# A hybrid attention layer on one core: an order that counts ScalarE's table loads, negated scores in one attention, and four token tiles in a weight buffer

## The chip, the cores and the metric

The kernel runs on 1 core of one Trainium2 chip. The metric is the time of one execution in microseconds (us) of device time, as the median of several runs; less is better. Beside it stands one execution recorded by the hardware profiler, with start and end of every instruction. The engines are PE (TensorE: matmuls and transposes; PEld is its weight load), DVE (VectorE), ACT (ScalarE), POOL (GpSimd) and SP (SyncE, which issues the DMAs here).

## The reference

One layer, applied to a prompt of 1024 tokens and to a sample of 32 tokens that has a cache of 512 older ones; model width 1024, all in float32. There are two attentions with 8 heads of 64 each: A is a softmax over a band of chunks with a learnt position bias, B is "stick-breaking", which is made of sigmoids and a running product.

```python
hn = rmsnorm(h, g_pre)
qA, kA, vA, gA, qB, kB, vB, gB = split(hn @ w_in)        # 8 times 512 columns
# A, per head: keys of the own 64-token chunk and the 8 chunks before
s  = qA @ kA.T * 64**-0.5 + bias[clip(k_pos - q_pos, -128, 128)]
oA = softmax(where(band, s, -1e30)) @ vA
# B, per head, strictly causal
z  = qB @ kB.T * 64**-0.5
after = sum over later causal keys of log_sigmoid(-z)
oB = where(causal, exp(log_sigmoid(z) + after), 0) @ vB
y  = concat(oA * silu(gA), oB * silu(gB)) @ w_out
h  = h + rmsnorm(y, g_post)
h  = h + sigmoid(h @ w_ple_gate) * (p @ w_ple)
```

The new keys and values are outputs too.

## The kernel before, in words

Tokens are taken as 9 tiles of 128 (the last holds the 32 of the sample); for the input projection they are regrouped into 3 column chunks of 352. Every float32 operand of a large matmul is split into a rounded high part and a low rest (`hi`, `lo`), and a product is three matmuls: high by high, high by low, low by high.

The work has three parts. **The start** (to about 60 us) loads the token tiles x0 to x8 (`load_x`), squares and scales them (`scale_x`), transposes them (`turn_x`) and makes the first projections qA, kA, vA of head pair 0. Tiles x0 to x2 and the later ones live in `ring0`, an arena with room for three such tiles; x3 and x4 live in a buffer `x34` that has the tag `wTh`, the place where the transposed attention weights go later. **The attention part** (to about 600 us) goes through eight stages, one for each pair of heads, in the order A0 B0 A1 B1 A2 B2 A3 B3. Within a stage two heads of one attention run (`attention`), while the projections of the next stage (or, in the last one, the gates) run between them as the dense work. In two A stages and two B stages the sample's attention is put in (`sample_attention`). **The last part** makes w_out and w_ple_gate with a seven-product Strassen scheme.

For one unit of attention, that is a head and a block of 128 queries, the steps are: scores on PE into one or two PSUM banks (tag `S`, three banks in all); in A, DVE adds the bias and takes the row maximum in one instruction (`tensor_tensor_reduce`, shown as CUSTOM_DVE_ANT_0 with its accumulator read), DVE negates that maximum, ACT takes the exponential with the negated maximum as bias, DVE takes a reciprocal, POOL multiplies; in B, ACT takes two sigmoids of the bank, DVE runs a product scan backwards over it, POOL multiplies. Then PE transposes the weights (`ptw`), ACT rounds them (`wTh`), DVE makes the rest (`wTl`), and PE multiplies with the values (`PV`).

ACT evaluates exponentials and sigmoids from tables, and an ACT_TABLE_LOAD stands in its queue wherever the one follows the other. Copies, casts and squares need no load of their own here.

The order of instructions is not that of the Python code. A `Recorder` takes down every operation with what it depends on, a planner (`order`) then simulates the five engines with fixed costs (`cost`) and emits for each engine a fixed queue: at each step the engine that can start first takes the ready operation of the lowest key, and on PE attention has class 0 and dense work class 1, so dense work fills the time in which no attention matmul is ready. An operation on another engine is counted as ready for PE only 400 ns late (`MARGIN`). All operations are emitted from one line of a helper, so the profile shows the one line L450 for nearly all of them and groups are told apart by the names of tiles.

Of the kernel before, what the change touches and what calls it, by code (L numbers as in the profile page):

```python
# [10 lines left out]
AF = mybir.ActivationFunctionType  # L11
ALU = mybir.AluOpType

P = 128
D = 1024
# [7 lines left out]
HD = 64  # L23
NEG = -1e30
# [148 lines left out]


class Op:
    __slots__ = ("eng", "what", "args", "kw", "key", "busy", "late", "ready", "left", "after", "at", "size", "shared")


LAND = {"PE": 165, "ACT": 0, "DVE": 0, "POOL": 0, "SP": 0, "CTL": 0}
SEM = 60  # L180
MARGIN = 400
ISSUE = 550
DMA_NS, DMA_RATE, DMA_MARGIN = 1500, 320.0, 2000
DVE_SET, POOL_SET = 137, 110

# [78 lines left out]
class Recorder:  # L264


    def __init__(self):
        self.ops, self.cls, self.low, self.closed, self.turns = [], 0, 0, [], []
        self.tensor = Engine(self, "PE", "tensor")
        self.vector = Engine(self, "DVE", "vector")  # L270
        self.scalar = Engine(self, "ACT", "scalar")
        self.gpsimd = Engine(self, "POOL", "gpsimd")
        self.sync = Engine(self, "SP", "sync")
# [26 lines left out]
    def node(self, eng, what, args, kw, after):  # L300
        o = Op()
        o.eng, o.what, o.args, o.kw, o.after = eng, what, args, kw, after
        o.key = (self.cls if eng == "PE" else self.low, len(self.ops))
        o.shared = False
        self.ops.append(o)
        return o

    def add(self, eng, what, args, kw):
        writes, reads = [], []
        method = what[1] if isinstance(what, tuple) else ""  # L310
        for i, a in enumerate(args):
            if isinstance(a, (View, Raw, Segments)):
                (writes if i == 0 or (method == "tensor_tensor_reduce" and i == 7) else reads).append(a)
        for k, a in kw.items():
            if isinstance(a, (View, Raw, Segments)):
                (writes if k in ("out", "accum_out") else reads).append(a)
        o = self.node(eng, what, args, kw, set())
        for mine, write in ((reads, False), (writes, True)):
            for v in mine:
                b = v.buf  # L320
                hit = False
                for other, box, wrote in b.uses:
                    if other is not o and (write or wrote) and all(p < y and x < q for (p, q), (x, y) in zip(v.box, box)):
                        o.after.add(other)
                        hit = True
                if b.pool is not None:
                    if not hit:
                        o.after.add(b.place)
                    b.pool.ops.append(o)
                b.uses.append((o, v.box, write))  # L330
        o.busy, o.late = self.cost(eng, method, args, kw, writes, reads)
        o.shared = eng == "POOL"
        if eng == "DVE":
            sbuf = [v for v in reads if isinstance(v, (View, Segments)) and not v.buf.psum and v.free() > 4]
            o.shared = len(sbuf) > 1 or (method == "tensor_copy" and len(sbuf) == 1 and not writes[0].buf.psum)
# [36 lines left out]
    def order(self):  # L372

        import heapq
        for place, old in self.turns:
            place.after.update(x[0] for x in old.uses)
        users = {id(o): [] for o in self.ops}
        for o in self.ops:
            o.left, o.ready = len(o.after), 0.0
            for a in o.after:  # L380
                users[id(a)].append(o)
        names = ("PE", "ACT", "DVE", "POOL", "SP", "CTL")
        free = dict.fromkeys(names, 0.0)
        soon = {e: [] for e in names}
        now = {e: [] for e in names}
        for o in self.ops:
            if not o.left:
                heapq.heappush(soon[o.eng], (0.0, o.key, id(o), o))
        out, port, line = [], 0.0, 0.0
        while len(out) < len(self.ops):  # L390
            best = None
            for e in names:
                if now[e]:
                    t = free[e]
                elif soon[e]:
                    t = max(free[e], soon[e][0][0])
                else:
                    continue
                if best is None or t < best[0]:
                    best = (t, e)  # L400
            t, e = best
            while soon[e] and soon[e][0][0] <= t:
                _, key, n, o = heapq.heappop(soon[e])
                heapq.heappush(now[e], (key, n, o))
            o = heapq.heappop(now[e])[2]
            if o.shared and e == "DVE" and port > t + DVE_SET:
                held = [x for x in now[e] if not x[2].shared]
                if held:
                    heapq.heappush(now[e], (o.key, id(o), o))
                    pick = min(held)  # L410
                    now[e].remove(pick)
                    heapq.heapify(now[e])
                    o = pick[2]
            o.at = t
            if e == "CTL":
                done = t
            elif e == "SP":
                free[e] = t + o.busy
                line = max(line, t + o.busy + DMA_NS) + o.late
                done = line + DMA_MARGIN  # L420
            else:
                if o.shared:
                    t = max(t, port - (DVE_SET if e == "DVE" else POOL_SET))
                    port = t + o.busy
                free[e] = t + o.busy
                done = t + o.busy + o.late
            out.append(o)
            for u in users[id(o)]:
                if u.eng == e and e != "SP":
                    r = t if e == "CTL" else free[e]  # L430
                else:
                    r = done + (0 if u.eng == "CTL" else SEM + (MARGIN if u.eng == "PE" else 0))
                u.ready = max(u.ready, r)
                u.left -= 1
                if not u.left:
                    heapq.heappush(soon[u.eng], (u.ready, u.key, id(u), u))
        return out
# [18 lines left out]
def stream_step(  # L456
# [108 lines left out]
    def load_x(t):  # L565
        n = min(P, T - t * P)
        if t == 3:
            x34.append(at.tile([P, ringh.cols], F32, tag="wTh", name="x34"))
        xt = x34[0][:, (t - 3) * D:(t - 2) * D] if 3 <= t < 5 else ring0.tile([P, D], f"x{t}")
        dma(xt[0:n], x_prompt[0, t * P:t * P + n, :] if t < 8 else x_sample[0])  # L570
        return xt, n

# [33 lines left out]
    def bias_rows():  # L606

        rb = ring0.tile([8, 257], "rb")
        dma(rb, rel_bias[0])
        R = ring1.tile([8, 768], "R")  # L610
        nc.gpsimd.memset(R, 0.0)
        nc.vector.tensor_scalar(R[:, 256:768], R[:, 256:768], rb[:, 0:1], None, ALU.add)
        nc.vector.tensor_copy(R[:, 0:256], rb[:, 0:256][:, ::-1])
        dma(r_dr, R)

# [96 lines left out]
    def col_steps(j):  # L712
# [7 lines left out]
        def mms(c, part):  # L720
# [24 lines left out]
                nc.gpsimd.tensor_tensor(sg, sg, box["og"], ALU.mult)  # L745
                dma(og_dr[n, :, cs], sg)
            elif k == "q":
                nc.scalar.activation(box["st"][:, cs], acc, AF.Copy, scale=SCALE)
            else:
                nc.scalar.copy(box["st"][:, cs], acc)  # L750

# [26 lines left out]
    def attention(ab, p, h):  # L778
# [5 lines left out]
        def begin():  # L784
            if ab == "A":
                bias = at2.tile([P, 640], F32, tag="bias", name=f"bias{nm}", bufs=2)
                dma(bias, bias_src(2 * p + h, P, 0, 640))
                nc.gpsimd.memset(bias[0:HD, 0:HD], NEG)
                nc.gpsimd.memset(bias[HD:P, 576:640], NEG)
                box["bias"] = bias  # L790

        def lo_block(i):
# [20 lines left out]
        def scores(i):  # L813
# [27 lines left out]
            else:  # L841
                m = small.tile([P, 4], F32, tag="stat", name=f"stat{nm}_{i}", bufs=6)
                for j, (a, b, s) in enumerate(pieces):
                    nc.vector.tensor_tensor_reduce(
                        w0[:, a:b], s, box["bias"][:, n - b:n - a][:, ::-1], 1.0,
                        -3e38 if j == 0 else m[:, j - 1:j], ALU.add, ALU.max, m[:, j:j + 1])
                last = len(pieces) - 1
                nc.vector.tensor_scalar(m[:, 2:3], m[:, last:last + 1], -1.0, None, ALU.mult)
                nc.scalar.activation(w1[:, 0:n], w0[:, 0:n], AF.Exp, bias=m[:, 2:3], accum_out=m[:, 3:4])
                nc.vector.reciprocal(m[:, 3:4], m[:, 3:4])  # L850
                nc.gpsimd.tensor_scalar(w1[:, 0:n], w1[:, 0:n], m[:, 3:4], 1.0, ALU.mult, ALU.mult)
            state[i] = w0, w1
# [96 lines left out]
    def sample_attention(ab, gi):  # L949
# [45 lines left out]
        def scores():  # L995
# [20 lines left out]
            else:  # L1016
                m = small.tile([P, 4], F32, tag="stat", name="stat" + nm, bufs=6)
                for j, (a0, b0, s) in enumerate(pieces):
                    nc.vector.tensor_tensor_reduce(
                        w0[:, a0:b0], s, bx["bias"][:, NK - b0:NK - a0][:, ::-1], 1.0,  # L1020
                        -3e38 if j == 0 else m[:, 0:1], ALU.add, ALU.max, m[:, j:j + 1])
                nc.vector.tensor_scalar(m[:, 2:3], m[:, 1:2], -1.0, None, ALU.mult)
                nc.scalar.activation(w1[:, 0:NK], w0[:, 0:NK], AF.Exp, bias=m[:, 2:3], accum_out=m[:, 3:4])
                nc.vector.reciprocal(m[:, 3:4], m[:, 3:4])
                nc.gpsimd.tensor_scalar(w1[:, 0:NK], w1[:, 0:NK], m[:, 3:4], 1.0, ALU.mult, ALU.mult)
            bx["w1"] = w1
# [829 lines left out]
```

## Time and profile before

| | us |
|---|---|
| median of 3 runs (lowest to highest) | 794.32 (794.28 to 794.92) |
| time of the profiled execution | 794.5 |
| its span from the first to the last instruction | 792.7 |
| around the span | 1.8 |
| PE busy | 778.6 |
| ACT busy, DVE busy, POOL busy | 537.3, 587.4, 470.1 |

A busy time is the union of the recorded durations. A matmul's recorded end is modelled and lies later than the start of the next one, so that a short wait of PE hides in the overlap; the start times are what is measured. In a timeline row the first number is the start in us from the span's start, the second the duration in us, and the bracket at the end is the idle time before it and what ended it. In a group of instructions, "x12 | 15.4, 1283 | 0.9" is 12 instructions, 15.4 us together, 1283 ns on average and 0.9 us of idle time before them.

### The profile page before, as it was taken

How to read it: one execution, taken by the hardware profiler on the slowest of the kernel's cores; microseconds unless marked ns; L12 is line 12 of the kernel's file. 1: busy time of each engine (PE TensorE's matmuls, PEld its weight loads, DVE VectorE, ACT ScalarE, POOL GpSimd, SP SyncE). 2: the span in 40 equal slices, each digit the busy share in tenths (PEclk: the TensorE clock that was granted, in tenths of full speed). 3: DMA queues.
4: the chain of work that ended last, by engine and by line, in shares of the span. 5: the costliest groups of instructions: out<-in, count | busy, mean ns of one | idle time of the engine just before them, and what ended most of it. 6: DMA issues, size and time to landing. Idle time of an engine off the chain costs nothing.

```text
span 792.7 us, 14512 instructions
## 1 busy us (share of the span) xinstructions
PE 778.6 (98%) x4606; PEld 717.9 (91%) x4606; DVE 587.4 (74%) x1170; ACT 537.3 (68%) x1173; POOL 470.1 (59%) x554
## 2 busy tenths in 40 slices
PE   8999999999999999999999999999999999999997
PEld 7999999899989998999998999999998787888786
DVE  7717778787778686877867788767565677988965
ACT  6636786786797677887766778664436976777551
POOL 5625867675777677454635246657462529599533
PEclk9999999999999999999999999999999999999999
DMA  8419866767866858544514746756589866859853
GB/s 296 138 49 289 215 188 213 189 189 226 229 192 205 232 176 238 144 128 123 142 54 132 172 111 175 225 167 188 151 261 291 282 190 186 288 168 336 272 170 133
DMA packets 161087, 153.66 MB, mean 194 GB/s; under 512 B 38562, under 2 KB 127178, under 8 KB 161011
## 3 DMA queue, kind: packets, MB, share of 16 engines
q1 hardware_dynamic: 161010, 152.73, 64.5%
q8 instruction: 37, 0.61, 0.3%
q14 instruction: 40, 0.32, 0.1%
HBM read 94.45 MB, written 49.83 MB: 182 GB/s over the span
## 4 chain that ended last, share of the span: by engine, by line
PE 84%; ACT 5%; DMA 3%; POOL 3%; DVE 3%; issue 2%; SPq 1%; DVEq 0%; ACTq 0%; POOLq 0%
PE mm_gA L450 6%; PE mm_gB L450 5%; PE mm_qB L450 5%; PE mm_vA L450 5%; PE mm_kB L450 5%; PE mm_qA L450 5%; PE PVB L450 4%; PE mm_kA L450 4%; PE SB L450 3%; PE mm_vB L450 3%; PE PVA L450 3%; PE SA L450 3%; PE g1P L450 2%; PE o3P L450 2%; PE o1P L450 2%; PE g0P L450 2%
## 5 line engine op out<-in xcount | busy, mean ns | idle before, releaser
L450 POOL TENSOR_TENSOR be<-be,om 128x1024 f32<-128x1024 f32 (+8 forms) x66 | 80.3, 1221 | 67.4 <-DVE om L450 34.0
L450 DVE TENSOR_TENSOR_SCAN om<-om,SB 128x384 f32<-128x384 f32 (+5 forms) x96 | 92.2, 966 | 14.5 <-ACT be L450 5.5
L450 POOL TENSOR_SCALAR be<-be,statA 128x640 f32<-128x640 f32 (+3 forms) x64 | 43.9, 691 | 52.8 <-DVE statA L450 37.0
L450 ACT ACTIVATE om<-SB 128x384 f32<-128x384 f32 (+5 forms) x96 | 46.6, 497 | 20.1 <-DVE SB L450 15.6
L450 ACT ACTIVATE be<-SB 128x384 f32<-128x384 f32 (+5 forms) x96 | 46.5, 498 | 13.4 <-DVE om L450 7.2
L450 ACT ACTIVATE be<-om,statA 128x640 f32<-128x640 f32 (+3 forms) x64 | 44.6, 697 | 15.5 <-DVE statA L450 11.3
L450 DVE TENSOR_TENSOR wTl<-ptwA,wTh 128x512 fp32r<-128x512 f32 (+2 forms) x80 | 36.2, 480 | 9.2 <-ACT wTh L450 8.9
L450 ACT CAST wTh<-ptwA 128x512 fp32r<-128x512 f32 (+2 forms) x80 | 32.1, 426 | 12.1 <-PE ptwA L450 10.4
L450 DVE TENSOR_TENSOR wTl<-ptwB,wTh 128x512 fp32r<-128x512 f32 (+3 forms) x64 | 33.7, 546 | 4.7 <-ACT wTh L450 4.3
L450 DVE CUSTOM_DVE_ANT_0 om<-SA,biasA 128x320 f32<-128x320 f32 (+2 forms) x64 | 30.9, 483 | 7.2 <-PE SA L450 5.6
L450 ACT CAST wTh<-ptwB 128x512 fp32r<-128x512 f32 (+3 forms) x64 | 29.6, 482 | 9.2 <-PE ptwB L450 5.9
L450 DVE TENSOR_TENSOR wTl<-be,wTh 128x640 fp32r<-128x640 f32 (+1 forms) x24 | 30.2, 1257 | 7.5 <-ACT wTh L450 7.4
L450 PE MATMUL SB<-kdB,LB 128*128 128x384 f32 (+5 forms) x96 | 33.4, 350 | 0.6 <-DVE om L450 0.6
L450 PE MATMUL SB<-klB,LB 128*128 128x384 f32 (+5 forms) x96 | 33.1, 347 | 0.0
L450 PE MATMUL ptwA<-ident,be 128*128 128x128 f32 x200 | 32.1, 273 | 0.5 <-DVE wTl L450 0.5
L450 PE MATMUL SA<-kdA,LA 128*128 128x320 f32 (+2 forms) x96 | 30.2, 323 | 1.7 <-DVE statA L450 0.9
L450 PE MATMUL ptwB<-ident,be 128*128 128x128 f32 x192 | 29.7, 274 | 0.6 <-POOL be L450 0.6
L450 PE MATMUL SA<-klA,LA 128*128 128x320 f32 (+2 forms) x96 | 29.1, 314 | 0.0
L450 POOL TENSOR_TENSOR oB<-oB,oB 128x256 f32<-128x256 f32 x32 | 25.5, 813 | 5.2 <-issue 3.5
L450 POOL TENSOR_TENSOR gB<-gB,gB 128x256 f32<-128x256 f32 x32 | 26.0, 837 | 2.4 <-DMA gB<-in_w_ple_gate_dram 1.8
L450 DVE TENSOR_TENSOR SB<-SB,maskb 128x128 f32<-128x128 f32 x64 | 17.6, 290 | 12.6 <-PE SB L450 10.0
L450 PEld LDWEIGHTS ptwA<-ident,be 128*128 128x128 f32 x200 | 24.2, 140 | 1.9 <-issue 1.0
(712 smaller groups left out, 2691.8 us busy)
## 6 DMA issues: line engine op xcount, KB each, us to landing
oB<-in_w_out_dram SPq DMA_DIRECT2D x16, 256.0 KB, 4.7
sum_dro<-oB SPq DMA_DIRECT2D x16, 256.0 KB, 2.4
gB<-in_w_ple_gate_dram SPq DMA_DIRECT2D x16, 256.0 KB, 3.8
sum_drg<-gB SPq DMA_DIRECT2D x16, 256.0 KB, 3.1
x<-in_x_prompt_dram SPq DMA_DIRECT2D x16, 256.0 KB, 4.6
h_dr<-h SPq DMA_DIRECT2D x8, 512.0 KB, 4.4
ht<-h_dr SPq DMA_DIRECT2D x8, 512.0 KB, 5.2
raw<-sum_drg SPq DMA_DIRECT2D x16, 256.0 KB, 3.5
```

Of the source, the lines that this page charges most:

```text
L450: getattr(getattr(tc.nc, o.what[0]), o.what[1])(*args, **kw)
```

## The change

Four edits in one diff. The planner now remembers which table ACT holds and adds 1280 ns when an exponential follows a sigmoid or the reverse. Each such operation is noted in the order of recording, and as soon as the kind changes, every operation of the new kind gets all operations of the run before as predecessors; so ACT can't begin the sigmoids of a B stage before the last exponential of the A stage ahead of it. The scores of A are kept with the opposite sign: q of A is scaled with -SCALE, the bias row is negated once after its load, the masked corners get +1e30, the reduction is a minimum instead of a maximum, the exponential has scale -1.0 and takes the minimum as its bias, and the instruction that negated the maximum goes. And the tokens' tiles x5 and x6 lie in `x34` beside x3 and x4.

```diff
--- before.py
+++ after.py
@@ -173,13 +173,14 @@
 
 
 class Op:
-    __slots__ = ("eng", "what", "args", "kw", "key", "busy", "late", "ready", "left", "after", "at", "size", "shared")
+    __slots__ = ("eng", "what", "args", "kw", "key", "busy", "late", "ready", "left", "after", "at", "size", "shared", "table")
 
 
 LAND = {"PE": 165, "ACT": 0, "DVE": 0, "POOL": 0, "SP": 0, "CTL": 0}
 SEM = 60
 MARGIN = 400
 ISSUE = 550
+TABLE = 1280
 DMA_NS, DMA_RATE, DMA_MARGIN = 1500, 320.0, 2000
 DVE_SET, POOL_SET = 137, 110
 
@@ -265,6 +266,7 @@
 
 
     def __init__(self):
+        self.with_table, self.old_table = [], []
         self.ops, self.cls, self.low, self.closed, self.turns = [], 0, 0, [], []
         self.tensor = Engine(self, "PE", "tensor")
         self.vector = Engine(self, "DVE", "vector")
@@ -301,7 +303,7 @@
         o = Op()
         o.eng, o.what, o.args, o.kw, o.after = eng, what, args, kw, after
         o.key = (self.cls if eng == "PE" else self.low, len(self.ops))
-        o.shared = False
+        o.shared, o.table = False, None
         self.ops.append(o)
         return o
 
@@ -328,6 +330,13 @@
                         o.after.add(b.place)
                     b.pool.ops.append(o)
                 b.uses.append((o, v.box, write))
+        if method == "activation" and args[2] in (AF.Exp, AF.Sigmoid):
+
+            o.table = args[2]
+            if self.with_table and self.with_table[-1].table != o.table:
+                self.old_table, self.with_table = self.with_table, []
+            self.with_table.append(o)
+            o.after.update(self.old_table)
         o.busy, o.late = self.cost(eng, method, args, kw, writes, reads)
         o.shared = eng == "POOL"
         if eng == "DVE":
@@ -386,7 +395,7 @@
         for o in self.ops:
             if not o.left:
                 heapq.heappush(soon[o.eng], (0.0, o.key, id(o), o))
-        out, port, line = [], 0.0, 0.0
+        out, port, line, table = [], 0.0, 0.0, AF.Exp
         while len(out) < len(self.ops):
             best = None
             for e in names:
@@ -419,6 +428,8 @@
                 line = max(line, t + o.busy + DMA_NS) + o.late
                 done = line + DMA_MARGIN
             else:
+                if e == "ACT" and o.table not in (None, table):
+                    t, table = t + TABLE, o.table
                 if o.shared:
                     t = max(t, port - (DVE_SET if e == "DVE" else POOL_SET))
                     port = t + o.busy
@@ -566,7 +577,7 @@
         n = min(P, T - t * P)
         if t == 3:
             x34.append(at.tile([P, ringh.cols], F32, tag="wTh", name="x34"))
-        xt = x34[0][:, (t - 3) * D:(t - 2) * D] if 3 <= t < 5 else ring0.tile([P, D], f"x{t}")
+        xt = x34[0][:, (t - 3) * D:(t - 2) * D] if 3 <= t < 7 else ring0.tile([P, D], f"x{t}")
         dma(xt[0:n], x_prompt[0, t * P:t * P + n, :] if t < 8 else x_sample[0])
         return xt, n
 
@@ -607,6 +618,7 @@
 
         rb = ring0.tile([8, 257], "rb")
         dma(rb, rel_bias[0])
+        nc.vector.tensor_scalar(rb, rb, -1.0, None, ALU.mult)
         R = ring1.tile([8, 768], "R")
         nc.gpsimd.memset(R, 0.0)
         nc.vector.tensor_scalar(R[:, 256:768], R[:, 256:768], rb[:, 0:1], None, ALU.add)
@@ -745,7 +757,7 @@
                 nc.gpsimd.tensor_tensor(sg, sg, box["og"], ALU.mult)
                 dma(og_dr[n, :, cs], sg)
             elif k == "q":
-                nc.scalar.activation(box["st"][:, cs], acc, AF.Copy, scale=SCALE)
+                nc.scalar.activation(box["st"][:, cs], acc, AF.Copy, scale=SCALE if ab == "B" else -SCALE)
             else:
                 nc.scalar.copy(box["st"][:, cs], acc)
 
@@ -785,8 +797,8 @@
             if ab == "A":
                 bias = at2.tile([P, 640], F32, tag="bias", name=f"bias{nm}", bufs=2)
                 dma(bias, bias_src(2 * p + h, P, 0, 640))
-                nc.gpsimd.memset(bias[0:HD, 0:HD], NEG)
-                nc.gpsimd.memset(bias[HD:P, 576:640], NEG)
+                nc.gpsimd.memset(bias[0:HD, 0:HD], -NEG)
+                nc.gpsimd.memset(bias[HD:P, 576:640], -NEG)
                 box["bias"] = bias
 
         def lo_block(i):
@@ -843,10 +855,9 @@
                 for j, (a, b, s) in enumerate(pieces):
                     nc.vector.tensor_tensor_reduce(
                         w0[:, a:b], s, box["bias"][:, n - b:n - a][:, ::-1], 1.0,
-                        -3e38 if j == 0 else m[:, j - 1:j], ALU.add, ALU.max, m[:, j:j + 1])
+                        3e38 if j == 0 else m[:, j - 1:j], ALU.add, ALU.min, m[:, j:j + 1])
                 last = len(pieces) - 1
-                nc.vector.tensor_scalar(m[:, 2:3], m[:, last:last + 1], -1.0, None, ALU.mult)
-                nc.scalar.activation(w1[:, 0:n], w0[:, 0:n], AF.Exp, bias=m[:, 2:3], accum_out=m[:, 3:4])
+                nc.scalar.activation(w1[:, 0:n], w0[:, 0:n], AF.Exp, bias=m[:, last:last + 1], scale=-1.0, accum_out=m[:, 3:4])
                 nc.vector.reciprocal(m[:, 3:4], m[:, 3:4])
                 nc.gpsimd.tensor_scalar(w1[:, 0:n], w1[:, 0:n], m[:, 3:4], 1.0, ALU.mult, ALU.mult)
             state[i] = w0, w1
@@ -1018,9 +1029,8 @@
                 for j, (a0, b0, s) in enumerate(pieces):
                     nc.vector.tensor_tensor_reduce(
                         w0[:, a0:b0], s, bx["bias"][:, NK - b0:NK - a0][:, ::-1], 1.0,
-                        -3e38 if j == 0 else m[:, 0:1], ALU.add, ALU.max, m[:, j:j + 1])
-                nc.vector.tensor_scalar(m[:, 2:3], m[:, 1:2], -1.0, None, ALU.mult)
-                nc.scalar.activation(w1[:, 0:NK], w0[:, 0:NK], AF.Exp, bias=m[:, 2:3], accum_out=m[:, 3:4])
+                        3e38 if j == 0 else m[:, 0:1], ALU.add, ALU.min, m[:, j:j + 1])
+                nc.scalar.activation(w1[:, 0:NK], w0[:, 0:NK], AF.Exp, bias=m[:, 1:2], scale=-1.0, accum_out=m[:, 3:4])
                 nc.vector.reciprocal(m[:, 3:4], m[:, 3:4])
                 nc.gpsimd.tensor_scalar(w1[:, 0:NK], w1[:, 0:NK], m[:, 3:4], 1.0, ALU.mult, ALU.mult)
             bx["w1"] = w1
```

## The prediction, made before the changed kernel was run

> **What bounds the kernel now.** I read the head of the page first: engine shares and the shares of the chain that ended last.
>
> ```profile
> span 792.7 us, 14512 instructions
> PE 778.6 (98%) x4606; PEld 717.9 (91%) x4606; DVE 587.4 (74%) x1170; ACT 537.3 (68%) x1173; POOL 470.1 (59%) x554
> ...
> PE 84%; ACT 5%; DMA 3%; POOL 3%; DVE 3%; issue 2%; SPq 1%; DVEq 0%; ACTq 0%; POOLq 0%
> ```
>
> PE is busy for 778.6 of 792.7 us and the chain lies 84% on it. The matmuls are the same before and after the change, so what can move is PE's idle time, 14.1 us of the span with the stretches before the first matmul and behind the last. The profiled execution took 794.5 us, 0.2 above the median of 794.32. The second view is PE's waits (in total, times, longest).
>
> ```profile
> PE mm_kB L450 <- ACT stvA L450: 1.6, 1, 1.6
> PE idle L450 <- DVE newh L450: 1.3, 1, 1.3
> PE PVB L450 <- DVE wTl L450: 1.3, 1, 1.3
> PE SA L450 <- DVE statA L450: 0.9, 2, 0.7
> PE SA L450 <- DVE LA L450: 0.8, 1, 0.8
> PE SB L450 <- DVE om L450: 0.6, 1, 0.6
> PE ptwB L450 <- POOL be L450: 0.6, 1, 0.6
> PE ptx L450 <- DVE be L450: 0.6, 2, 0.3
> PE ple L450 <- ACT wph0True L450: 0.5, 1, 0.5
> PE ptwA L450 <- DVE wTl L450: 0.5, 1, 0.5
> PE PVA L450 <- DVE be L450: 0.2, 1, 0.2
> ```
>
> These are 8.9 us, and they limit the gain. The first (1.3, before the warm-up matmuls) and those on wph0True (0.5) and ptx (0.6) lie in the start, that on LA (0.8) where attention begins. The others, 5.7 us, lie in the attention part, and the question is which of them come from table loads. The groups of ACT give those:
>
> ```profile
> L450 ACT ACT_TABLE_LOAD x12 | 15.4, 1283 | 0.9 <-PEq L1844 0.7
> ```
>
> One load opens the program; eight stages that alternate need seven more; the other four are to and fro. The timeline shows what a load does. First the longest wait, at the beginning of A3, on ACT and then on PE:
>
> ```profile
> 418.43 1.05 ACT L450 CAST LA<-stqA 64x1024 fp32r<-64x1024 f32 x1
> 419.49 1.28 ACT L450 ACT_TABLE_LOAD   x1
> 420.79 0.40 ACT L450 ACTIVATE be<-om,statA 128x128 f32<-128x128 f32 x1
> 421.19 0.43 ACT L450 COPY stvA<-mm_vA 128x352 f32<-128x352 f32 x1
> ```
>
> ```profile
> 353.31 1.46 PE L450 MATMUL mm_vB<-hnl,wh_vB 128*128 128x352 f32 x8
> 354.61 0.64 PE L450 MATMUL mm_vB<-hnh,wh_vB 128*128 128x352 f32 x3
> ...
> 418.65 1.43 PE L450 MATMUL mm_kB<-hnl,wh_kB 128*128 128x352 f32 x8
> 421.67 1.55 PE L450 MATMUL mm_kB<-hnh,wh_kB 128*128 128x352 f32 x8 [1.59 <-ACT stvA L450]
> ```
>
> PE's next chunk of mm_kB needs a bank that ACT empties with the copy at 421.19. In ACT's queue the load and an exponential stand ahead of it. The old planner had no 1.28 us for the load, so it thought the copy would come that much earlier. Eight matmuls in a row take 1.30 from first start to the next start (353.31 to 354.61), 0.16 each, so those from 418.65 make room at 419.95; the next starts at 421.67, 1.7 us late where the view says 1.6: the waits are a little longer than listed. Now the other places, ACT and then DVE:
>
> ```profile
> 228.52 1.28 ACT L450 ACT_TABLE_LOAD   x1
> 229.82 0.83 ACT L450 ACTIVATE be<-om,statA 128x640 f32<-128x640 f32 x1
> ...
> 310.02 1.28 ACT L450 ACT_TABLE_LOAD   x1
> ...
> 352.61 1.28 ACT L450 ACT_TABLE_LOAD   x1
> 354.21 0.36 ACT L450 COPY otA<-PVA 64x256 f32<-64x256 f32 x1
> ```
>
> ```profile
> 230.77 0.16 DVE L450 RECIPROCAL statA<-statA 128x1 f32<-128x1 f32 x1 [1.16 <-ACT be L450]
> ...
> 310.04 0.16 DVE L450 RECIPROCAL statA<-statA 128x1 f32<-128x1 f32 x1 [1.78 <-ACT be L450]
> ...
> 354.60 0.43 DVE L450 TENSOR_TENSOR otA<-PVA,otA 64x256 f32<-64x256 f32 x1 [1.66 <-ACT otA L450]
> ```
>
> Before 230.77 DVE was idle for 1.16, waiting for the sum of the exponential of 229.82, which stood behind the load of 228.52; behind that reciprocal in DVE's queue stands the scan that frees a score bank, and PE's wait on om (0.6) follows, then the one on be (0.2). At 310.04 it is the same: DVE idle 1.78 behind ACT, the bias addition late, PE waiting on statA (0.7) and then, past two more loads, on ptwB's operand (0.6). At 354.60 DVE has waited 1.66 for the copy behind the load of 352.61, and PE waits for wTl (0.5). So 1.6 + 0.6 + 0.2 + 0.7 + 0.6 + 0.5 = 4.2 us of the 5.7 are behind a load that the planner did not know of. The largest of the rest is not:
>
> ```profile
> 148.09 4.09 DVE L450 TENSOR_TENSOR wTl<-be,wTh 128x896 fp32r<-128x896 f32 x1
> ```
>
> Four microseconds for 896 elements, where 256 in 0.43 (at 354.60) would make it 1.5. Whatever held DVE up here, no load stood ahead of it.
>
> **The change part by part.** *Fewer loads.* The order of the changed kernel, listed without running it, has 8 loads for 12; those at 228.52, 232.28, 310.02 and 312.42 are gone. On ACT that is 4 x 1.28 = 5.1 us of 537, which is worth nothing by itself, as ACT isn't the bound. What it is worth is the waits at those two places: 0.6 + 0.2 and 0.7 + 0.6, 2.1 us. [...]
>
> *Loads known to the planner.* The seven at the stage changes remain, with the opening one, but the order is now made with 1280 ns for each, against 1283 measured. At A3 the new order has the last score matmul of B2 twelve dense matmuls earlier, with the same queue on ACT behind it less one weight cast, so the copy comes about 1.9 us earlier against PE (12 x 0.16) and the 1.6 us should be gone; at B2 the copy of the value product stands before the load, not behind it, which takes away the 0.5. I value this at 2.1 us; its bounds are 0 (the wait turns up again at the next consumer) and 2.1.
>
> *The wait that it adds.* No sigmoid may start before the last exponential of the stage ahead. Behind the waiting instruction on ACT stand its casts and PSUM copies; the planner sees the dependency and places them. It costs PE only if the three score banks are full and dense work or another bank is missing as well; see the second rival.
>
> *Negated scores.*
>
> ```profile
> L450 DVE TENSOR_SCALAR statA<-statA 128x1 f32<-128x1 f32 x64 | 9.5, 149 | 1.2
> ```
>
> 64 (and two for the sample) DVE steps of 0.15 us go, 9.8 us of DVE's 587. Each stands between bias addition and exponential, and ahead of the next bias addition, which frees a bank. DVE is the engine that ends four of the waits above, but not by this step; outside them dense matmuls cover it. I count 0, bounds 0 to 0.5 gained. The one new step (the bias row of 8x257 negated, an estimate of 0.43 as for the 256 elements of 354.60) lies in the start, some 20 us ahead of the first scores in the listed order; cost 0.
>
> *Four tiles in the weights' room.* x5 and x6 are asked for right behind x4 instead of after tiles of the ring are free, on SP's queue they pass the four small copies of the mask, which the sample's attention needs much later; x7 and the sample's tile move ahead of both halves of wr_vA, and POOL takes the reciprocal root of x6 before the second half of vA's weights.
>
> ```profile
> 25.91 0.57 POOL L450 TENSOR_TENSOR rs<-rs,halfp 128x1 f32<-128x1 f32 x1
> 26.43 0.61 POOL L450 CAST wTl<-wr_vA 128x512 fp32r<-128x512 f32 x1
> 27.12 1.30 POOL L450 TENSOR_TENSOR wTl<-wr_vA,wTl 128x512 fp32r<-128x512 f32 x1
> ...
> 28.36 0.19 ACT L450 ACTIVATION_READ_ACCUMULATOR be<-om 128x1 f32 x1
> ...
> 29.70 1.78 PE L450 MATMUL mm_vA<-hnh,wTl 128*128 128x352 f32 x10
> ```
>
> PE starts vA at 29.70 and needs that second half at its fifth matmul, near 30.35. POOL is free at 28.42; the root of x6 has to await the sum that ACT gives at 28.55, and takes 0.57 and a shorter step ahead of it, then 0.61 for the cast: near 30.1. That is just in time; I take 0, bounds 0 to 1 us lost. Nothing in the start gains, since PE waits there for DVE and not for x5.
>
> *What is redrawn.* On all engines the order differs after about 25 us, up to the last stage's gates. The waits that have nothing to do with loads (1.3 on PVB and about 0.2 of the statA row, 1.5 us in 530 us of attention) belong to one order, and another order has its own. In that length the old order has one collision like that of 148.09; I allow the new one two, less the smaller waits: 2.5 instead of 1.5, 1.0 us lost. Bounds: 1.5 gained (none) and 4 lost (four of them).
>
> **The sum.** Against the profiled 794.5: -2.1 - 2.1 + 1.0 = -3.2; the start times show each of the six waits to be 0.1 to 0.15 longer than listed, -0.7. That is 790.6, and 790.4 against the median.
>
> **The rivals.** *The waits only move.* Four loads less, but PE has to wait elsewhere for as much: redrawn waits at their bound of 4 lost, or the start late by 1 and half of the known loads' 2.1 not had. For it: the wait on PVB, as large as any at a load, came of no load. Against it: two places with four loads make 2.1 us of waits in 12 us of time, the rest of the attention part 1.5 in more than 500. Time 793.5 to 795, say 794.3.
>
> *The strict order of the sets starves PE at the four A-to-B changes* (slower). Behind the last exponential come the load, two sigmoids, and a scan until the first score bank is free:
>
> ```profile
> L450 DVE TENSOR_TENSOR_SCAN om<-om,SB 128x384 f32<-128x384 f32 (+5 forms) x96 | 92.2, 966 | 14.5 <-ACT be L450 5.5
> L450 ACT ACTIVATE om<-SB 128x384 f32<-128x384 f32 (+5 forms) x96 | 46.6, 497 | 20.1 <-DVE SB L450 15.6
> ```
>
> 1.28 + 2 x 0.50 + 0.97 = 3.3 us, in which three banks hold scores that none can read. In the new order PE has between the first and the fourth score bank of B3 19 dense matmuls, 3.1 us, and 8 value products, 7 transposes and 4 score matmuls, another 2.3 as an estimate by their columns against the dense ones' 352, so about 5.4; at B0 and B2 more. So it decides from about 2 us of backlog on ACT when the first bank is written: an operand cast (1.05, as at 418.43) with an exponential (0.83, at 229.82) would reach it. If that held everywhere by 1.5 us too much, 4 x 1.5 = 6.0 are added to 790.4: 796.4. Against it: the planner now counts load and dependency both, and adds 400 ns for PE.
>
> *The gain is larger.* Everything in the attention part, 5.7 us and the understatement of 0.7 goes: 788.0.
>
> **How the numbers follow.** About 0.2%, 1.6 us, is what a measurement of this kernel can tell from no change. My forecast, with the larger gain as its end, has 0.66; the moved waits 0.21; the starved PE 0.13. The range goes from the larger gain to a little over the moved waits, 787.8 to 795.4, and leaves out most of the starved case. Faster by over 0.2% (under 792.7) takes the forecast's 0.66 and a little of the moved waits that end below, 0.67; the same 0.19; slower (over 795.9) 0.14. That the change doesn't do what it says is left out, as the listed order shows the eight loads.
>
> **What would show it.** Right: 8 loads in ACT's groups, 5.1 us less there; statA's TENSOR_SCALAR gone from DVE; PE's view of waits without om, stvA and ptwA near the stage changes and its sum below 6 us; PE's busy time nearly as before with the span shorter by the waits. The moved waits would show as a sum near 9 with other names, the starved PE as waits of SB on om or on ACT's be at four places. A wait of mm_vA on wTl near 30 us shows that the start is late. The prediction is wrong if the waits at the stage changes stay though the load is planned, or if PE's listed waits outside them pass 4 us.

## The result, and the profile after

| | before | after |
|---|---|---|
| median (lowest to highest), us | 794.83 (794.28 to 795.02) | 788.80 (788.55 to 791.73) |
| span of the profiled execution, us | 792.7 | 789.9 |

The three executions of the kernel before that stand above are among its five here. The ratio is 0.9935, with a 95% interval of 0.9921 to 0.9949: 6.0 us less by the medians, and 5.2 by the ratio, which counts every execution. Forecast were 3.9. The profiled execution of the changed kernel is the longest of its five, 791.73; the others took 788.55 to 789.77. Its page begins so, with the shares of the chain that ended last under the engines:

```profile
span 789.9 us, 14445 instructions
PE 777.9 (98%) x4606; PEld 718.7 (91%) x4606; DVE 590.3 (75%) x1105; ACT 532.2 (67%) x1169; POOL 472.3 (60%) x554
...
PE 86%; DVE 3%; ACT 3%; DMA 3%; POOL 2%; issue 1%; SPq 1%; ACTq 0%; DVEq 0%
```

ACT has lost 5.1 us. DVE is 2.9 us busier, although 65 of its instructions are gone: others have become longer (two steps of 128x32 that make Kl0sA, for instance, take 3.1 us together instead of 0.4). PE's waits and ACT's loads:

```profile
PE ptwA L461 <- POOL om L461: 1.4, 1, 1.4
PE idle L461 <- DVE newh L461: 1.3, 1, 1.3
PE ptkA L461 <- DVE wTl L461: 1.0, 1, 1.0
PE mm_kB L461 <- ACT stvA L461: 1.0, 1, 1.0
PE ptx L461 <- DVE be L461: 0.8, 2, 0.6
PE SA L461 <- DVE LA L461: 0.8, 1, 0.8
PE ptwB L461 <- DVE wTl L461: 0.2, 1, 0.2
PE ptwA L461 <- DVE wTl L461: 0.2, 1, 0.2
```

```profile
L461 ACT ACT_TABLE_LOAD x8 | 10.3, 1283 | 0.8 <-PEq L1854 0.7
```

Eight loads, as listed. The waits add up to 6.7 us instead of 8.9. The names SB on om, SA on statA, PVA on be and ptwB on POOL are gone, and what is left right behind a load is one wait on stvA. It isn't the one of A3; there the timeline of ACT and of PE now reads:

```profile
416.26 1.28 ACT L461 ACT_TABLE_LOAD   x1
417.56 0.40 ACT L461 ACTIVATE be<-om,statA 128x128 f32<-128x128 f32 x1
...
417.96 0.43 ACT L461 COPY stvA<-mm_vA 128x352 f32<-128x352 f32 x1
...
417.55 1.43 PE L461 MATMUL mm_kB<-hnl,wh_kB 128*128 128x352 f32 x8
418.82 0.48 PE L461 MATMUL mm_kB<-hnh,wh_kB 128*128 128x352 f32 x2
```

The same load, exponential and copy stand in the same order as before, but the copy ends at 418.39, before PE asks for the bank: from 417.55 to 418.82 there are 1.27 us for eight matmuls, and no wait. At B2 the copy of the value product (otA, 351.93) now stands ahead of the load (352.31), as forecast, and the wait of 0.5 there is gone. The wait on stvA in the list lies at the beginning of A1, behind a load that the planner knew of:

```profile
174.71 1.28 ACT L461 ACT_TABLE_LOAD   x1
176.00 0.40 ACT L461 ACTIVATE be<-om,statA 128x128 f32<-128x128 f32 x1
...
176.40 0.79 ACT L461 COPY stvA<-mm_vA 128x352 f32<-128x352 f32 x2
...
174.77 1.13 PE L461 MATMUL mm_vA<-hnl,wh_vA 128*128 128x352 f32 x6
176.89 1.40 PE L461 MATMUL mm_kB<-hnh,wh_kB 128*128 128x352 f32 x7 [0.98 <-ACT stvA L461]
```

### The profile page after: what moved, and what is told of

Read it like the earlier page. It is cut to its first block, busy times and chain, and to the rows that moved or that the text cites. A ratio compares the mean times of both kernels' runs of the same rounds, so it can differ in the third digit from the quotient of the medians.

```text
span 789.9 us, 14445 instructions
## 1 busy us (share of the span) xinstructions
PE 777.9 (98%) x4606; PEld 718.7 (91%) x4606; DVE 590.3 (75%) x1105; ACT 532.2 (67%) x1169; POOL 472.3 (60%) x554
## 4 chain that ended last, share of the span: by engine, by line
PE 86%; DVE 3%; ACT 3%; DMA 3%; POOL 2%; issue 1%; SPq 1%; ACTq 0%; DVEq 0%
PE mm_gB L461 6%; PE mm_gA L461 6%; PE mm_kB L461 5%; PE mm_qA L461 5%; PE mm_kA L461 5%; PE mm_vA L461 5%; PE mm_qB L461 5%; PE PVB L461 4%; PE mm_vB L461 4%; PE SA L461 4%; PE SB L461 4%; PE PVA L461 3%; PE ptwB L461 3%; PE g1P L461 2%; PE o3P L461 2%; PE o1P L461 2%
## 5 line engine op out<-in xcount | busy, mean ns | idle before, releaser
L461 POOL TENSOR_TENSOR be<-be,om 128x256 f32<-128x256 f32 (+8 forms) x66 | 81.6, 1240 | 66.2 <-DVE om L461 51.9
L461 ACT CAST wTh<-be 128x640 fp32r<-128x640 f32 (+1 forms) x24 | 19.2, 799 | 8.2 <-DMA be<-swapA 5.3
```

Of the source, the lines that this page charges most:

```text
L461: getattr(getattr(tc.nc, o.what[0]), o.what[1])(*args, **kw)
```

## The experiments

Three theories were tried. **T**: loads to and fro, and loads that the planner doesn't know of, make PE wait, and the table edits take that away. **N**: the shorter chain on DVE (no negation) brings the gain. **R**: the changed planner merely draws another order, and an order has its own waits, so that the time falls or rises by luck. A redrawn order is one in which the planner has placed the instructions anew.

### The table edits alone, and everything but them

The first kernel is the kernel before with the planner's 1280 ns and the rule on predecessors. The second is the changed kernel without these two:

```diff
-                if e == "ACT" and o.table not in (None, table):
-                    t, table = t + TABLE, o.table
...
-            o.after.update(self.old_table)
```

> The kernel before with the two table edits alone (the 1280 ns in the planner and the rule that each kind of table work waits for the run before it); scores not negated, two tiles in the weights' room as before. It has 8 loads. Theory T (fewer and planned loads take PE's waits away): most of the change's 6.0 us, 789 to 791 against a kernel before of 794.8. Theory N (DVE's relief by the negated scores brings it): 793.5 or more. Theory R (any redrawn order gives another time, and the new one is lucky): anywhere from 789 to 798, without relation to the number of loads.

> The changed kernel without the two table edits: scores negated, four tiles in the weights' room, the planner knows nothing of loads. It has 14 loads, two more than before. T: no gain, 794 to 797, about 1 us for each pair of loads to and fro (2.1 us for two pairs before). N: 789 to 791. R: anywhere from 789 to 798.

Measured: 793.54, ratio 0.9986 (0.9976 to 0.9995), and 797.91, ratio 1.0043 (1.0031 to 1.0055). The second speaks for T and against N: with negated scores and four tiles but 14 loads the kernel is slower than before, by 0.9 us more than T gave it. R allows either time. Its loads can be seen at work at the beginning of B0, on ACT and on PE:

```profile
104.36 1.28 ACT L450 ACT_TABLE_LOAD   x1
105.65 0.28 ACT L450 ACTIVATE om<-SB 128x128 f32<-128x128 f32 x1
...
106.32 1.28 ACT L450 ACT_TABLE_LOAD   x1
107.62 0.83 ACT L450 ACTIVATE be<-om,statA 128x640 f32<-128x640 f32 x1
...
109.03 1.28 ACT L450 ACT_TABLE_LOAD   x1
110.32 0.28 ACT L450 ACTIVATE be<-SB 128x128 f32<-128x128 f32 x1
...
107.42 0.75 PE L450 MATMUL ptwA<-ident,be 128*128 128x128 f32 x4 [0.52 <-DVE wTl L450]
...
109.06 0.85 PE L450 MATMUL PVA<-wTh,v2A 128*128 128x512 f32 x4 [0.58 <-ACT wTh L450]
110.65 0.67 PE L450 MATMUL SB<-kdB,LB 128*128 128x512 f32 x1 [0.73 <-ACT be L450]
```

Three loads in 5 us, and three waits of PE. But the first kernel doesn't fit T: eight planned loads, and 1.2 us gained instead of 4 to 6; its 793.5 lies in the readings of N and of R. Its profiled execution is the longest of its eleven (792.33 to 795.80), but the largest wait in it has no load near: ACT stood for 2.77 us for a DMA of stvA, and PE for ACT:

```profile
318.51 1.04 ACT L461 COPY vtA<-stvA 128x1024 f32<-128x1024 f32 x1 [2.77 <-DMA stvA<-swapA]
...
319.85 0.41 PE L461 MATMUL ptwA<-ident,be 128*128 128x128 f32 x2 [1.92 <-ACT vtA L461]
```

### The same orders without loads

To part the price of the loads from an order's own waits, the order must stay. In these kernels every engine keeps its queue exactly; only the function changes when the instruction is emitted, and ACT_TABLE_LOAD stands x2 in ACT's groups, 2.6 us together, where the order before has x12 with 15.4 and the changed one x8 with 10.3:

```diff
-                args = [a.get() if isinstance(a, (View, Raw, Segments)) else a for a in o.args]
+                args = [a.get() if isinstance(a, (View, Raw, Segments)) else AF.Sigmoid if a is AF.Exp else a for a in o.args]
```

> The kernel before in exactly its own order on every engine, but every exponential is evaluated as a sigmoid, so that only two loads (in the first 65 us) are left of twelve; A's weights are not a softmax. T: the six waits behind loads go and little comes in their place: 4.2 us by the view of waits, 4.9 by the start times, so 789.9 to 790.6 against 794.8. R: the waits turn up at the next consumer, and the fall is under 2 us.

> The changed kernel in exactly its own order, with exponentials evaluated as sigmoids (two loads left of eight; A's weights are not a softmax). T: its order has room for the loads, so that only the wait of mm_kB on stvA at the beginning of A1 (1.15 us) can go: 787.6 to 788.8. R: a fall of 2 us or more, as large as in the order before, would say that the planner's knowledge of loads is not what helped.

> The kernel with the table edits alone (793.5), in exactly its own order, with exponentials evaluated as sigmoids: two loads left of eight; A's weights are not a softmax. In its trace two of PE's waits stand behind a load (mm_kB on stvA, 1.5 us in A1 and 0.5 in A3); the largest others do not (ptwA behind a copy of vtA that waited for a DMA, 2.1 us, and mm_vA on wh_vA, 1.4). Theory T (loads cost PE what their listed waits say): 791 to 792. Theory R (what this order lost against the changed kernel, 4.7 us, is the order's own and no load's): not below 790.5, so at least 2 us above the changed kernel without loads (788.6). If the loads still cost this order as much as the order before (5.4), 788.2.

> The kernel with negated scores and four tiles but without the table edits (797.9), in exactly its own order, with exponentials evaluated as sigmoids: two loads left of fourteen; A's weights are not a softmax. T: its waits near the stage changes add up to 7.7 us by the start times (107 to 111, 178, 230 to 238, 316 to 320, 421, 480 us), so about 790. R: 793 or more, the rest being the order's own.

The medians are 789.4 for the order before and 788.6 for the changed one, both as T has it to 0.5 us; 793.1 for the table edits alone, above T's range and within R's; and 788.6 without the table edits, 1.4 below T's and far below R's. They stand once more in the table below. The substitute takes as long as the exponential. This is the group of the kernel before, and the same group in its order without loads:

```profile
L450 ACT ACTIVATE be<-om,statA 128x640 f32<-128x640 f32 (+3 forms) x64 | 44.6, 697 | 15.5 <-DVE statA L450 11.3 <-DVE wTl L450 3.9
```

```profile
L450 ACT ACTIVATE be<-om,statA 128x640 f32<-128x640 f32 (+3 forms) x64 | 44.6, 697 | 16.5 <-DVE statA L450 11.2 <-DVE wTl L450 4.4 <-DVE Vl2sA L450 0.5
```

PE's waits in the order before, without its loads:

```profile
PE PVB L450 <- DVE wTl L450: 1.3, 1, 1.3
PE idle L450 <- DVE newh L450: 1.3, 1, 1.3
PE ptx L450 <- DVE be L450: 0.8, 2, 0.6
PE SA L450 <- DVE LA L450: 0.8, 1, 0.8
PE mm_kB L450 <- ACT stvA L450: 0.3, 1, 0.3
PE SB L450 <- DVE om L450: 0.3, 1, 0.3
```

All six waits that the prediction put down to loads are gone or down to 0.3; the 1.3 on PVB, which it said was none of a load's, stands. The span fell from 792.7 to 787.8: 4.9 us, as much as the prediction's 4.2 and 0.7. Since PE's queue is the same, the start of each matmul can be set against its start in the other execution, and this tells where the time went. 1.0 us is gained from 225 to 240 us (times of the order before), 2.0 from 306 to 318, 0.7 from 350 to 360 and 1.3 from 415 to 424, 5.0 at the four places to which the prediction had traced its six waits. The start lost 0.5, and a place near 335 without a load gained 0.5; everywhere else the two executions run alike to 0.1 us, at the loads of 108, 173 and 477 us too, which thus cost PE nothing. The granted clock is 0.999 in both. In the changed kernel's order, the wait on stvA in A1 went too, but another came ten dense and four score matmuls later:

```profile
176.73 0.50 PE L461 MATMUL SA<-kdA,LA 128*128 128x512 f32 x1 [0.76 <-DVE statA L461]
```

So the length of a wait behind a load isn't yet the load's price: without the load, PE waited 0.76 at the next consumer instead of 0.98 at the copy.

### Other orders for the same work

```diff
-MARGIN = 400
+MARGIN = 410
```

> The changed kernel with the planner's allowance for PE at 410 ns instead of 400, which redraws the order and leaves the 8 loads and all work as they are. T: within 1.5 us of the changed kernel, 787.3 to 790.3. R: redrawn orders scatter by several us, anywhere from 787 to 795.

> The kernel before with the planner's allowance for PE at 410 ns instead of 400: another order, again 12 loads, all work the same. T: 793 to 797, since as many loads are unknown to the planner. R: anywhere from 789 to 798, and not above the redrawn changed kernel by more than the scatter.

> The changed kernel with the planner's allowance for PE at 390 ns instead of 400: one more redrawn order, again 8 loads. By the scatter of the redrawn orders so far (788.6, 789.4, 793.1 and, with planned loads, 788.8, 793.5, 798.0) anywhere from 788 to 798; below 790 would say that 798.0 is the exception, above 792 that 788.8 is a lucky order.

> The redrawn changed kernel of 798.0 in exactly its own order, with exponentials evaluated as sigmoids (two loads left of eight; A's weights are not a softmax). Theory T+R (planned loads cost nothing, what this order lost is its own): 796.5 to 798.0; its one large wait next to a load is SA on statA at 177.9 us, 0.8. If planned loads can cost as much as unplanned ones: 789 to 793.

> The redrawn kernel before of 798.2 in exactly its own order, with exponentials evaluated as sigmoids (two loads left of twelve; A's weights are not a softmax). T+R: the waits next to its loads go (SB on ACT at 110.8 us, 2.5; mm_kB on stvA at 177.8, 0.8; SB on om at 239.9, 0.8; SA on om and statA at 304.7 and 315.4, 0.8), 4 to 6 us: 792 to 794. If these waits are the order's own: 796.5 or more.

All together, medians in us, with the ratio to the kernel before and its interval; the loads' price is the difference of the two medians:

| order | loads | time | ratio | two loads | ratio | the loads' price |
|---|---|---|---|---|---|---|
| before | 12, unknown | 794.8 | 1 | 789.4 | 0.9945 (0.9929 to 0.9961) | 5.4 |
| before, margin 410 | 12, unknown | 798.2 | 1.0052 (1.0039 to 1.0065) | 793.0 | 0.9980 (0.9970 to 0.9989) | 5.2 |
| no table edits | 14, unknown | 797.9 | 1.0043 (1.0031 to 1.0055) | 788.6 | 0.9926 (0.9914 to 0.9939) | 9.3 |
| after | 8, planned | 788.8 | 0.9935 (0.9921 to 0.9949) | 788.6 | 0.9924 (0.9911 to 0.9937) | 0.2 |
| table edits alone | 8, planned | 793.5 | 0.9986 (0.9976 to 0.9995) | 793.1 | 0.9985 (0.9976 to 0.9994) | 0.5 |
| after, margin 410 | 8, planned | 798.0 | 1.0056 (1.0043 to 1.0070) | 798.4 | 1.0047 (1.0033 to 1.0062) | -0.4 |
| after, margin 390 | 8, planned | 790.1 | 0.9939 (0.9927 to 0.9950) | not run | | |

Two of the twelve executions behind 789.4 took 794.2 and 796.0; its ratio counts them and puts the loads' price there at 4.4.

Two things stand apart in this table. Read along the rows, T holds in every order that was run both ways: unknown loads cost 5 to 9 us, planned ones at most 0.5, which is within what can be measured. Read down the column of two loads, R holds too: the same work without loads takes from 788.6 to 798.4 us by its order alone. Ten nanoseconds of margin, which say nothing of the chip, cost the changed kernel 9 us. With the margin at 410 on both sides the same change is worth 0.2 us (798.2 to 798.0): the loads' price of 5.2 is gone, and the redrawn order takes it back (793.0 to 798.4). T's expectations, which held the order for nearly harmless, were missed with it: 787.3 to 790.3 for the changed kernel with margin 410 (798.0), at most 797 for the kernel before with it (798.2), 791 to 792 for the table edits without loads (793.1). R's reach was too short as well: at most 795 for the 798.0, at most 798 for the 798.2. The two redrawn orders without loads came out as T and R together had it, 793.0 within 792 to 794, and 798.4 just above 796.5 to 798.0. The run with margin 390, 790.1, fell between the two readings that were set for it. It is nearer to the changed kernel than to its other redrawing.

The waits of the order with margin 410 show what such luck is made of. The largest comes from DVE and POOL; first DVE, then POOL, then PE:

```profile
147.15 2.55 DVE L461 TENSOR_TENSOR wTl<-be,wTh 128x640 fp32r<-128x640 f32 x1
149.62 2.05 DVE L461 TENSOR_TENSOR_SCAN om<-om,SB 128x384 f32<-128x384 f32 x2
...
146.20 2.82 POOL L461 TENSOR_TENSOR oB<-oB,oB 128x256 f32<-128x256 f32 x4
...
151.73 0.41 PE L461 MATMUL SB<-kdB,LB 128*128 128x320 f32 x1 [1.71 <-DVE om L461]
```

DVE's step of 640 elements took 2.55 us and ended 0.7 us after POOL's four steps, which began ahead of it; the scans behind it freed the score bank late. Others are for a cast of wh_vA (1.5), for two of wh_kB (1.9 together), for wTh and v2B (1.2 and 1.0). None of these lies within 7 us of a load, and in the same order without loads they stand again (1.4 for om, then 1.5, 1.3, 1.4 and 1.0).

### The negation put back

The changed kernel in its own order, with a DVE step in each of the 66 places, on which the exponential waits:

```diff
+                if o.copy:
+                    to, fro = (x.get() for x in o.copy)
+                    tc.nc.vector.tensor_scalar(to, fro, 1.0, None, ALU.mult)
```

> The changed kernel in exactly its own order, with a DVE step put back in each of the 66 places where the negation stood (it copies the minimum, and the exponential takes the copy as its bias); the planner doesn't know of it. DVE gets 66 x 0.149 = 9.8 us more. The prediction's step (the negation is worth 0 to 0.5 us): 788.8 to 789.3. Theory N (the relief of DVE brings a good part of the 6 us): 791 or more.

Measured: 789.36, ratio 0.9930 (0.9918 to 0.9943), against 788.80 and 0.9935 without. The steps are there:

```profile
L466 DVE TENSOR_SCALAR statA<-statA 128x1 f32<-128x1 f32 x64 | 9.8, 154 | 2.2
```

DVE became 8.1 us busier (590.3 to 598.4), and the time moved by less than the two intervals can tell apart. N falls for this order. This execution, in the same order, also shows why the changed kernel's profiled one was long: here PE's longest wait of the list, 1.4 on POOL's om near 118 us, is missing, as it is in the same order without loads. The step of DVE that it hung on, in the changed kernel and then in this one:

```profile
116.02 1.14 DVE L461 TENSOR_TENSOR wTl<-be,wTh 128x640 fp32r<-128x640 f32 x1 [1.60 <-ACT wTh L461]
```

```profile
113.93 1.04 DVE L461 TENSOR_TENSOR wTl<-be,wTh 128x640 fp32r<-128x640 f32 x1
```

It came 2.1 us later in the profiled execution, behind ACT's cast of be at 115.26 (113.17 in the other one, where the trace names a DMA of be as what it waited for). Why it was late that time isn't settled; but the order doesn't have this wait each time, and 791.73 is not what it usually takes.

## Why the prediction was right, by its own steps

**Sign and range** held: 788.80 lies between 787.8 and 795.4, 1.6 under the 790.4. Through the two orders without loads the 6.0 us split into 5.4 - 0.2 = 5.2 for the loads and 789.4 - 788.6 = 0.8 for all the rest.

**Fewer and known loads** were put at 2.1 + 2.1, with 0.7 for the understatement of the listed waits: 4.9. The runs say 5.2 by the medians. By the ratios it is 3.5 (0.55% for the order before less 0.11% for the one after), and their intervals, some 0.3% wide, hold both. The mechanism is shown by the pairs of runs, and the six waits are the right ones. By place, the order before gains 1.0 + 2.0 = 3.0 us where loads go to and fro (near 230 and 310) and 0.7 + 1.3 = 2.0 at the two later stage changes, where 2.1 each, and their part of the 0.7, were put. But what of this is worth having fewer loads, and what planning them, isn't shown: no order with the one alone was run.

**What is redrawn** was the mis-sized term: 1.0 lost was allowed, and 0.8 gained was measured, together with negation and tiles. Of the 2.1 us by which the gain was larger than forecast, 1.8 are this and 0.3 the loads. The 0.8 by itself isn't clear of noise (0.9945 and 0.9924, with intervals that overlap). More important is its range. I set it at 1.5 gained to 4 lost, from the one collision of 148.09 in 530 us. Five other orders without loads lay between 0.8 below and 9.0 above the order before without loads. With the margin at 410 the same change would have ended at 798.0, outside the range and on the other side. Of the four orders with planned loads that were run, two are faster than before by over 0.2%, one lies within it and one is slower: the range, and the chance of 0.67 for faster, left this term too little room. That the order drawn at 400 was a good one, and the time so within the range, was luck; what the loads gave was not.

**Negated scores** at 0 to 0.5: borne out within what can be measured (0.6 between the medians, with overlapping intervals of the ratios). **Four tiles** at 0 to 1 lost: no wait of mm_vA on wTl stands in the view, and the first vA starts at 29.85 for 29.70, so the start wasn't late; the tiles alone were not run.

**The rivals.** *The waits only move* was given 794.3; it comes near to what happened with the table edits alone (793.5), where waits for a DMA and for a cast of wh_vA (1.9 and 1.3 us in the view) stand in the place of the loads'. *The strict order starves PE* didn't occur: in the views of the changed kernel and of the table edits alone no wait of SB is listed, and the one of the margin at 410 lies in the midst of B0. *The larger gain*, 788.0, lies nearest to the result.

**The signs** were mixed. Eight loads and the missing step of DVE are there, and ACT is 5.1 us less busy. But a wait on stvA at a stage change was to be gone, and a new one of 1.0 stands in A1. The sum of the listed waits forecast as under 6 was 6.7, of which 1.4 belong to that one execution. Waits outside the stage changes were not to pass 4 us: in the attention part they are 2.8, and with the start's 2.9 they would be 5.7. The sign didn't say which was meant; counted with the start, the kernel before had passed it already, with 4.7.

**The price of a load on ACT**, 1.28 us a piece in the forecast's 5.1, is what the runs show: 12 loads less, from 14 to 2 in the order without table edits, took ACT's busy time from 540.2 to 525.0, which is 1.27 each. In the rows of that kernel at 104 to 107 us a load starts within 20 ns of the end of the instruction ahead (a cast, 105.83 + 0.48 to 106.32), as the next one does behind a load (104.36 + 1.28 to 105.65).

## What to carry to other kernels

Here a cost that the planner didn't know reached the end by four to six tenths, even on an engine that is busy for two thirds of the time (5.4 us for ten loads of 1.28, 9.3 for twelve); grouped and planned, the loads that were left hid (0.2 us for six). But an edit to such a planner draws a new order, and the order alone was worth up to 10 us here. To learn what a cost is worth, take it out in a fixed order; to learn what an edit to the planner is worth, draw several orders on both sides before a single difference is believed.

## What was not expected of the hardware

The 4.09 us of DVE at 148.09 in the kernel before, left open in the prediction, fall together with a run of POOL's:

```profile
146.60 2.51 POOL L450 TENSOR_TENSOR be<-be,om 128x256 f32<-128x256 f32 x3
149.07 0.73 POOL L450 TENSOR_TENSOR oB<-oB,oB 128x256 f32<-128x256 f32 x1
149.75 0.09 POOL L450 MEMSET om<- 128x1 f32 x1
149.80 1.43 POOL L450 TENSOR_TENSOR oB<-oB,oB 128x256 f32<-128x256 f32 x2
```

Apart from a MEMSET of 0.09, POOL ran steps with two inputs from 146.60 to 151.23 without a pause, and DVE's step, which also has two inputs, ended at 152.18. The same shape took 1.09 us with the table edits alone, where POOL stood idle until 322.02:

```profile
321.09 1.09 DVE L461 TENSOR_TENSOR wTl<-be,wTh 128x896 fp32r<-128x896 f32 x1 [2.76 <-ACT wTh L461]
```

In the two places shown DVE's step ended 0.95 and 0.7 us after a run of POOL's that had begun ahead of it, and took longer than its shape did elsewhere: 3.0 us longer here (4.09 for 1.09), and some 1.5 at 147.15 above (2.55 for the 1.04 at 113.93). It doesn't outlast such a run each time: in the kernel before, DVE's step of 640 elements at 141.79 took 1.75 us and ended 0.7 after the one POOL step that was running (to 142.85), while POOL's next step (142.80 to 144.14) was under way; and with the margin at 410 the step of 896 elements at 152.18 took 1.17 while two steps of POOL's with two inputs ran (151.53 to 154.30). What decides this isn't known, and no run took POOL's steps away, so the cause isn't shown.
